# One chain of norms for eight row blocks, begun inside the attention, with new places for some roundings and subtractions, on one Trainium2 core

## The chip, the core and the metric

The kernel runs on one core of a Trainium2 chip. The core has a matrix engine (PE, with a separate row PEld for its weight loads), VectorE (DVE), ScalarE (ACT), GpSimd (POOL) and SyncE (SP), whose queue issues the DMAs. Each engine works through its own list of instructions in order; semaphores make one wait for another. The metric is the device time of one execution in microseconds (us), as the median of several runs. All detailed times come from one execution that the hardware profiler recorded.

## What is computed

One decoder layer on x of 1024 rows by 1024 columns in float32. The change lies where the first half of the layer (mixers and output projection) passes into the second (norm and MLP):

```python
    merged = jax.nn.sigmoid(gate_a) * o_gdn + jax.nn.sigmoid(gate_b) * o_att
    x = x + merged @ w_out

    h2 = rms_norm(x, norm_mlp_g)
    x = x + jnp.square(jax.nn.relu(h2 @ w_mlp_up)) @ w_mlp_down
    return x

def rms_norm(x, g):
    xf = x.astype(jnp.float32)
    y = xf * lax.rsqrt(jnp.mean(xf * xf, axis=-1, keepdims=True) + EPS)
    return (y * g.astype(jnp.float32)).astype(x.dtype)
```

`o_gdn` comes from a gated delta rule and `o_att` from an attention in which each query keeps 256 selected keys; `w_mlp_up` is 1024 by 4096. The gain g of the norm is multiplied into the up weights, so the kernel only scales each row by its root.

## The kernel before

**Row blocks.** The 1024 rows are eight blocks of 128. The attention goes through them in the order 0, 7, 1, 6, 2, 3, 5, 4, each in two groups of four heads (`g` = 0, 1): scores `s` on PE, a softmax on VectorE (`mx`, `nm`, `pr`) and ScalarE (`pr`), transposes `pt` of the probabilities on PE, their rounding into a high part `ph` (ScalarE) and a low part `pl` (VectorE), and the product `o` with the values. The output projection follows each block (PE, name `dd`). `residual` adds it into the block's row buffer, writes the rows to HBM by a DMA on SP's queue (`XD`, 512 KB; the last stage reads them back) and sums the squares on ScalarE.

**Names of buffers.** The row buffers are called `w` with a number: blocks 0, 1, 2, 3 are `w_11064`, `w_11166`, `w_11267`, `w_11327`; blocks 5, 6, 7 are `w_11364`, `w_11207`, `w_11119`; block 4, the last, is `w_11402`. `ident` is the identity for transposes; `pt` and `s` are two rings of two PSUM banks each; `m` are slots of merged activations and weights; `hh` and `ha` are high parts, `hl` and `la` low parts of a rounded operand.

**Norm.** `roots` turns the sum of squares into a reciprocal root with 11 VectorE instructions of one to three elements per partition (`nms`, `nr`, `n2t`): the mean, a first guess and three Newton steps. `norm2` does it for blocks 0, 1, 2 and then for 3, scales each block in place once its XD write is through (the first 512 columns on VectorE, the others on ScalarE), and turns the first half of the rows by eight groups of four transposes, which `norm_out` rounds (`ha`, `la`). `early` does the same for blocks 6, 7 and for 5, and forms on VectorE what a product scheme with seven instead of eight products needs of the second half of the rows (t1 to t4, sums and differences of halves, in place). `early_columns` transposes the columns of blocks 5, 6, 7 for two of these sets, in groups of three, which `early_rounded` rounds with 384 elements. `norm2b` treats block 4: its roots, its parts of t1, t2, t3, and in one go t4 of all four blocks.

**What sets the order.** The program is a set of generators with a priority each (a low number goes first). The planner `Weave` keeps a clock for every engine, adds an assumed cost for each instruction, and steps the best generator whose conditions are met. `yield "V"` means: wait until VectorE is free; `yield ("xd", tb)`: until the planned arrival of that write. The order so planned is fixed for each engine. The first lines of a generator's stretch up to the next `yield` are planned together, and a step's end (`wv.t`) is that of the latest of its instructions. Nearly all instructions are issued by one helper, L2203, so the trace shows one line for all of them, and names have to serve in place of lines. After the last selection of keys the planner also counts the port that VectorE and GpSimd share (`wv.shared`).

Of the kernel before, what the change touches and what calls it, by code (L numbers as in the profile page):

```python
# [14 lines left out]
AF = mybir.ActivationFunctionType  # L15
OP = mybir.AluOpType
# [9 lines left out]
HALF = 512  # L26
# [24 lines left out]
def body(tc, a, out, dbg=None):  # L51
    nc = tc.nc
    ctx = ExitStack()
    V, A, G, PE, SY = nc.vector, nc.scalar, nc.gpsimd, nc.tensor, nc.sync
# [43 lines left out]
    wv = Weave(tc)  # L98
# [3 lines left out]
    def rsq_w(pl, dst, src, n, tag, apart=True):  # L102
        t = pl.tile([P, max(n, 4)], F32, name=tag + "t")[:, :n]
        V_.tensor_scalar(dst.bitcast(I32), src.bitcast(I32), -0.5, float(0x5F3759DF), op0=OP.mult, op1=OP.add)
        for _ in range(3):
            if apart:
                yield
            V_.scalar_tensor_tensor(t, dst, -0.5, src, op0=OP.mult, op1=OP.mult)
            if apart:
                yield  # L110
            V_.tensor_tensor(t, t, dst, op=OP.mult)
            if apart:
                yield
            V_.scalar_tensor_tensor(dst, t, 1.5, dst, op0=OP.add, op1=OP.mult)
# [80 lines left out]
    def after(key):  # L195
        wv.add(0, later(wv.busy["SY"] + SY_LATENCY, key))
# [1216 lines left out]
    def residual(qb, pw):  # L1413
        yield ("x", qb)
        yield 0.2
        for c in range(2):
            cs = slice(c * HALF, (c + 1) * HALF)
            V_.tensor_tensor(x1[qb][:, cs], x1[qb][:, cs], pw[c], op=OP.add)
        yield
        wv.done("x1", qb)  # L1420
        SY_.dma_start(XD[qb * P:(qb + 1) * P, :], x1[qb])
        after(("xd", qb))
        junk = tp.tile([P, D], BF16, name="th", bufs=2)
        A_.activation(junk, x1[qb], AF.Square, accum_out=nss[:, qb:qb + 1])
        yield
        wv.done("ss", qb)
# [9 lines left out]
        yield  # L1436
        wv.done("h2k", half, k)

    def roots(tbs):
        for tb in tbs:  # L1440
            yield ("ss", tb)
        bs = slice(min(tbs), max(tbs) + 1)
        V_.tensor_scalar(nms[:, bs], nss[:, bs], 1.0 / D, EPS, op0=OP.mult, op1=OP.add)
        yield from rsq_w(cst, nr[:, bs], nms[:, bs], len(tbs), "n2", apart=False)
        yield


    def norm2():
        tbs = [qb for qb, g in ATT if g and qb // 4 == first]
        for now in (tbs[:3], tbs[3:]):  # L1450
            yield from roots(now)
            for tb in now:
                yield ("xd", tb)
                for c, eng in enumerate("VA"):
                    yc = x1[tb][:, c * HALF:(c + 1) * HALF]
                    yield eng
                    if c:
                        A_.activation(yc, yc, AF.Copy, scale=nr[:, tb:tb + 1])
                    else:
                        V_.tensor_scalar(yc, yc, nr[:, tb:tb + 1], None, op0=OP.mult)  # L1460
        yield
        for c in range(2):
            ys = [x1[first * 4 + i][:, c * HALF:(c + 1) * HALF] for i in range(4)]
            for k in range(4 * c, 4 * c + 4):
                ring = (ss, ptr)[k % 2]
                yield ring.ready
                ps, slot_ = ring.get()
                for i in range(4):
                    PE_.transpose(ps[:, i * P:(i + 1) * P], ys[i][:, (k % 4) * P:(k % 4 + 1) * P], ident)
                wv.add(1, norm_out(first, k, ps, ring, slot_))  # L1470
            yield
            wv.done("turned", c)
# [5 lines left out]
    y22, comb, pairs = {}, {}, {}  # L1478
    places = {0: 0, 2: 2, 3: 4, 1: 6}

    def early(tbs):
        yield from roots(tbs)
        for tb in tbs:
            i, r = tb % 4, nr[:, tb:tb + 1]
            b11, b12 = part(first, 0)[i], part(1 - first, 0)[i]
            y22[i] = part(1 - first, 1)[i]
            yield ("xd", tb)
            yield "A"
            A_.activation(y22[i], y22[i], AF.Copy, scale=r)
            yield  # L1490
            yield ("turned", 0)
            yield "V"
            V_.scalar_tensor_tensor(b11, b12, r, b11, op0=OP.mult, op1=OP.subtract)
            yield "V"
            V_.scalar_tensor_tensor(b12, b12, r, y22[i], op0=OP.mult, op1=OP.subtract)
            yield
            wv.done("combined", i)

    def early_columns():
        js = [tb % 4 for tb in EARLIER]  # L1500
        for j in js:
            yield ("combined", j)
        yield ("wo", NA - 2)
        for m in (0, 2):
            if m:
                yield
                for j in js:
                    yield "V"
                    V_.tensor_tensor(y22[j], y22[j], part(first, 0)[j], op=OP.subtract)
                yield  # L1510
            for k in range(4):
                if k % 2 == 0:
                    pairs[m, k // 2] = [hpair(f"{n}{places[m] + k // 2}") for n in ("hh", "hl")]
                    for i in range(2):
                        comb[m, k + i] = [t[:, i] for t in pairs[m, k // 2]]
                ring = (ss, ptr)[k % 2]
                yield ring.ready
                ps, slot_ = ring.get()
                for j in js:
                    PE_.transpose(ps[:, j * P:(j + 1) * P], y22[j][:, k * P:(k + 1) * P], ident)  # L1520
                wv.add(2, early_rounded(m, k, ps, ring, slot_))
        yield
        wv.done("early")

    def early_rounded(m, k, ps, ring, slot_):
        cs = slice(min(EARLIER) % 4 * P, (max(EARLIER) % 4 + 1) * P)
# [25 lines left out]
    vl[1] = pA.tile([P, NB, P], F32R, name="vl1")  # L1552
    wv.add(1, vprep(1))
    wv.add(4, score())
    wv.add(0, loadm())
    wv.add(0, loadx())
    wv.add(1, wout_weights())
# [12 lines left out]

    wv.run(until=("pv", NA - 2))
    wv.add(8, norm2())
    for tbs in (EARLIER[1:], EARLIER[:1]):
        wv.add(2, early(tbs))
    wv.add(2, early_columns())


# [99 lines left out]
    def norm2b():  # L1677
        tb = ATT[-1][0]
        i, r = tb % 4, nr[:, tb:tb + 1]
        yield from roots([tb])  # L1680

        y = hpair("hh6", F32)[:, 0]
        t1, t4, t3, t2 = part(first, 0), part(first, 1), part(1 - first, 0), part(1 - first, 1)
        V_.tensor_scalar(y, t2[i], r, None, op0=OP.mult)
        yield
        yield ("early",)
        wv.add(0, last_columns(0, i, y))
        V_.scalar_tensor_tensor(t1[i], t3[i], r, t1[i], op0=OP.mult, op1=OP.subtract)
        yield ("T", 0, 3)
        V_.tensor_tensor(t2[i], y, t1[i], op=OP.subtract)  # L1690
        yield
        wv.add(0, last_columns(2, i, t2[i]))
        V_.scalar_tensor_tensor(t3[i], t3[i], r, y, op0=OP.mult, op1=OP.subtract)
        yield ("T", 2, 3)
        wv.add(1, columns(3, t3))
        yield "V"
        for j in range(4):
            V_.tensor_tensor(t4[j], t4[j], t2[j], op=OP.subtract)
        yield ("col", 3)
        wv.add(1, columns(1, t1))  # L1700
        yield ("col", 1)
        wv.add(1, columns(4, t4))

    def last_columns(m, i, row):
# [480 lines left out]
class _Ordered:  # L2185
# [12 lines left out]
    def __getattr__(self, op):  # L2198
        f = getattr(self.eng, op)
        name, wv = self.name, self.wv  # L2200

        def call(*args, **kw):
            ins = f(*args, **kw)  # L2203
            o = args[0] if args else kw["out"]
            n = 1
            for d in o.shape[1:]:
                n *= d
            if name == "PE":
                fast = op == "matmul" and args[1].dtype == F32R
                if op == "matmul" and not fast and "tile_position" not in kw:  # L2210
                    return wv.issue(name, ins, (n * 1.67 + 5) / 1e3, 0.25)
                if op == "matmul" and "tile_position" in kw:
                    return wv.issue(name, ins, 0.03, 0.25)
                return wv.issue(name, ins, (n * (0.417 if fast else 0.835) + (13.4 if wv.shared else 2.5)) / 1e3, 0.25)
            if name == "SY":
                return wv.issue(name, ins, max(0.5, n * o.shape[0] / 9e4), SY_LATENCY)
            if name == "A":
                return wv.issue(name, ins, 0.13 + n / 1200 + (0.1 if "accum_out" in kw else 0), 0.15)
            if name == "V":
                return wv.issue(name, ins, 0.07 + n / 960, 0.12, self.port(op, args, kw))  # L2220
            if op == "tensor_tensor":
                return wv.issue(name, ins, 0.33 + n / 476, 0.2, True)
            return wv.issue(name, ins, 0.15 + n / 1000, 0.2)
        return call
# [49 lines left out]
```

## Time and profile before

| | |
|---|---|
| median of 3 runs | 1806.71 us (1806.06 to 1808.27) |
| profiled execution | 1806.61 us, its span 1804.9 us |
| mean granted clock of PE | 0.998 of full |
| PE busy | 1783.6 us (99%) |
| VectorE busy | 1287.2 us (71%) |
| ScalarE busy | 1022.8 us (57%) |
| GpSimd busy | 533.3 us (30%) |
| chain that ended last, by engine | PE 93%, DVE 4%, ACT 1%, issue 1%, POOL 1% |

The span is the time from the first to the last recorded instruction; 1.7 us of the execution lie around it. The chain is followed back from the last instruction: at each step to the work that released it. PE is busy nearly throughout, so a gain must either take work off PE or fill the few holes in its list; the holes are found by listing the stretches in which it is idle, with the engine that ended each. Times in the rows below count from the span's start.

### The profile page before, as it was taken

How to read it: one execution, taken by the hardware profiler on the slowest of the kernel's cores; microseconds unless marked ns; L12 is line 12 of the kernel's file. 1: busy time of each engine (PE TensorE's matmuls, PEld its weight loads, DVE VectorE, ACT ScalarE, POOL GpSimd, SP SyncE). 2: the span in 40 equal slices, each digit the busy share in tenths (PEclk: the TensorE clock that was granted, in tenths of full speed). 3: DMA queues.
4: the chain of work that ended last, by engine and by line, in shares of the span. 5: the costliest groups of instructions: out<-in, count | busy, mean ns of one | idle time of the engine just before them, and what ended most of it. 6: DMA issues, size and time to landing. Idle time of an engine off the chain costs nothing.

```text
span 1804.9 us, 28444 instructions
## 1 busy us (share of the span) xinstructions
PE 1783.6 (99%) x10252; PEld 1517.6 (84%) x10252; DVE 1287.2 (71%) x2746; ACT 1022.8 (57%) x2186; POOL 533.3 (30%) x738
## 2 busy tenths in 40 slices
PE   9999999999999999999999999989999999999999
PEld 8999998888888888888888888768888888888887
DVE  5556768867877788875368677776766668969673
ACT  6566656656676554553457666666766664333331
POOL 0003530743362415753014121222323222222230
PEclk9999999999999999999999999999999999999999
DMA  5111242232222222232355221315445459473241
GB/s 165 50 47 47 71 129 65 50 97 77 66 64 71 53 65 69 75 86 75 95 186 183 76 90 53 114 38 184 167 152 170 135 185 363 133 250 122 100 136 52
DMA packets 192193, 198.80 MB, mean 110 GB/s; under 512 B 36738, under 2 KB 140467, under 8 KB 192051
## 3 DMA queue, kind: packets, MB, share of 16 engines
q1 hardware_dynamic: 192050, 196.97, 34.7%
q8 instruction: 81, 1.33, 0.3%
q14 instruction: 62, 0.50, 0.1%
HBM read 141.20 MB, written 55.74 MB: 109 GB/s over the span
## 4 chain that ended last, share of the span: by engine, by line
PE 93%; DVE 4%; ACT 1%; issue 1%; POOL 1%; DMA 0%; SPq 0%; ACTq 0%; POOLq 0%; DVEq 0%
PE dd L2203 55%; PE o L2203 15%; PE s L2203 7%; PE pt L2203 6%; PE tt L2203 3%; PE cc L2203 2%; PE sq L2203 2%; PE oo L2203 1%; PE jj L2203 1%; DVE w L2203 1%; DVE hl L2203 1%; DVE m L2203 0%; PE tp L2203 0%; DVE n2t L2203 0%; DMA pj<-in_x_dram 0%
## 5 line engine op out<-in xcount | busy, mean ns | idle before, releaser
L2203 PE MATMUL dd<-hh,w 128*128 128x512 f32 x1568 | 517.4, 401 | 0.0
L2203 PEld LDWEIGHTS dd<-hh,w 128*128 128x128 f32 x1568 | 289.0, 189 | 51.4
L2203 PE MATMUL dd<-hl,w 128*128 128x512 f32 x784 | 316.2, 403 | 0.9 <-DVE hl L2203 0.9
L2203 ACT ACTIVATE m<-m 128x512 f32<-128x512 f32 (+1 forms) x240 | 139.9, 625 | 79.3 <-PE dd L2203 34.3
L2203 PE MATMUL dd<-w,hh 128*128 128x256 f32 x960 | 179.4, 284 | 0.4 <-DVE w L2203 0.4
L2203 PE MATMUL dd<-hh,m 128*128 128x512 f32 x520 | 173.5, 398 | 0.7 <-DVE w L2203 0.5
L2203 DVE TENSOR_TENSOR m<-m,m 128x512 fp32r<-128x512 f32 (+2 forms) x184 | 143.3, 804 | 38.7 <-ACT m L2203 33.3
L2203 PEld LDWEIGHTS dd<-hl,w 128*128 128x128 f32 x784 | 147.8, 189 | 26.4 <-DVE hl L2203 1.4
L2203 PEld LDWEIGHTS dd<-w,hh 128*128 128x128 f32 x960 | 151.5, 191 | 1.5 <-DVE w L2203 0.6
L2203 PE MATMUL dd<-w,hl 128*128 128x256 f32 x480 | 136.2, 284 | 0.0
L2203 POOL TENSOR_TENSOR sx<-sx,stmp 128x60 f32<-128x60 f32 (+24 forms) x248 | 119.7, 483 | 19.4
L2203 PEld LDWEIGHTS dd<-hh,m 128*128 128x128 f32 x520 | 97.6, 190 | 20.4 <-DVE w L2203 2.0
L2203 POOL TENSOR_TENSOR stmp<-sx,um 128x60 f32<-128x60 f32 (+24 forms) x186 | 83.4, 448 | 89.5 <-DMA um<-ZA 61.8
L2203 POOL TENSOR_TENSOR m<-m,m 128x512 f32<-128x512 f32 x48 | 69.0, 1445 | 120.6 <-DVE m L2203 63.3
L2203 PE MATMUL dd<-hl,m 128*128 128x512 f32 x260 | 103.2, 397 | 0.9 <-POOL hl L2203 0.9
L2203 DVE TENSOR_SCALAR_CACHE_REDUCE tkeq<-sc,cand 128x384 f16<-128x384 f32 (+3 forms) x128 | 103.3, 807 | 1.0
L2203 ACT ACTIVATE hh<-m 128x1024 fp32r<-128x1024 f32 x44 | 45.1, 1056 | 90.0 <-PE s L2203 42.0
L2203 ACT ACTIVATE ha<-m 128x1024 fp32r<-128x1024 f32 x44 | 45.3, 1056 | 86.0 <-PE o L2203 34.9
L2203 PEld LDWEIGHTS dd<-w,hl 128*128 128x128 f32 x480 | 91.8, 191 | 0.6
L2203 DVE TENSOR_TENSOR w<-w,w 128x1024 fp32r<-128x1024 f32 (+1 forms) x63 | 71.0, 1130 | 22.5 <-ACT w L2203 21.7
L2203 ACT ACTIVATE tkcm<-sc,cand 128x896 f16<-128x896 f32 x64 | 70.0, 1094 | 28.3 <-DVE cand L2203 25.2
L2203 ACT ACTIVATE w<-w 128x1024 fp32r<-128x1024 f32 x48 | 50.8, 1058 | 53.9 <-PE dd L2203 53.7
(413 smaller groups left out, 4412.2 us busy)
## 6 DMA issues: line engine op xcount, KB each, us to landing
HD<-m SPq DMA_DIRECT2D x112, 256.0 KB, 2.3
m<-HD SPq DMA_DIRECT2D x56, 512.0 KB, 3.9
w<-in_w_in_dram SPq DMA_DIRECT2D x48, 512.0 KB, 4.0
m<-in_w_mlp_up_dram SPq DMA_DIRECT2D x33, 512.0 KB, 4.8
wraw<-in_w_in_dram SPq DMA_DIRECT2D x8, 1024.0 KB, 5.3
m<-in_w_mlp_down_dram SPq DMA_DIRECT2D x16, 512.0 KB, 7.4
w<-in_x_dram SPq DMA_DIRECT2D x10, 512.0 KB, 5.5
es<-GC SPq DMA_DIRECT2D x8, 512.0 KB, 4.9
```

What stands on the lines that cost most here:

```text
L2203: ins = f(*args, **kw)
```

## The change

- A new generator `norms` makes the roots of all blocks in one chain, in the order of the attention: (0, 7), (1, 6), (2, 3), (5). It is added with the attention itself, with priority 2. For the first two groups (`apart`) each of the small instructions is planned by itself, so that others can stand between them; `norm2b` still makes block 4's.
- A new generator `scaled` for each block scales both halves in place (the first 512 columns only for blocks 0 to 3) as soon as its roots are there and its XD write has arrived.
- `norm2` and `early` no longer make roots or scale; they wait for `("scaled", tb)`. `early` is now one generator per block, in the order 7, 6, 5.
- `early_rounded` has priority 0 in place of 2.
- t4 of blocks 5, 6, 7 is formed at the end of `early_columns`; `norm2b` forms block 4's alone, and later, behind set 1's transposes.
- In `residual` the planned end of a step no longer includes the issue of the XD write.
- In the planner, a VectorE instruction of under 16 elements per partition is put at 0.17 us plus its elements, not 0.07, while the port is shared.

The number of instructions is the same on every engine.

```diff
+        t = wv.t
         SY_.dma_start(XD[qb * P:(qb + 1) * P, :], x1[qb])
         after(("xd", qb))
+        wv.t = t
...
-    def roots(tbs):
+    def roots(tbs, apart=False):
...
-        bs = slice(min(tbs), max(tbs) + 1)
+        bs = slice(tbs[0], tbs[-1] + 1, max(1, tbs[-1] - tbs[0]))
...
+    def norms():
+        qbs = [qb for qb, g in ATT if g]
+        for n, grp in enumerate((qbs[0:2], qbs[2:4], qbs[4:6], qbs[6:7])):
+            yield from roots(sorted(grp), apart=n < 2)
+            for tb in grp:
+                wv.add(2, scaled(tb))
+
+    def scaled(tb):
+        yield ("xd", tb)
+        r = nr[:, tb:tb + 1]
+        for c, eng in enumerate("VA"):
+            yc = x1[tb][:, c * HALF:(c + 1) * HALF]
+            if eng == "A":
+                yield eng
+                A_.activation(yc, yc, AF.Copy, scale=r)
+            elif tb // 4 == first:
+                yield eng
+                V_.tensor_scalar(yc, yc, r, None, op0=OP.mult)
+        yield
+        wv.done("scaled", tb)
...
-                wv.add(2, early_rounded(m, k, ps, ring, slot_))
+                wv.add(0, early_rounded(m, k, ps, ring, slot_))
...
+        for j in js:
+            yield ("turned", 1)
+            yield "V"
+            t4 = part(first, 1)[j]
+            V_.tensor_tensor(t4, t4, y22[j], op=OP.subtract)
+        yield
+        wv.done("early", 4)
...
+    wv.add(2, norms())
...
-        yield "V"
-        for j in range(4):
-            V_.tensor_tensor(t4[j], t4[j], t2[j], op=OP.subtract)
         yield ("col", 3)
         wv.add(1, columns(1, t1))
         yield ("col", 1)
+        yield ("early", 4)
+        yield "V"
+        V_.tensor_tensor(t4[i], t4[i], t2[i], op=OP.subtract)
+        yield
         wv.add(1, columns(4, t4))
...
-                return wv.issue(name, ins, 0.07 + n / 960, 0.12, self.port(op, args, kw))
+                return wv.issue(name, ins, (0.17 if n < 16 and wv.shared else 0.07) + n / 960, 0.12, self.port(op, args, kw))
```

On VectorE, where the last block's softmax meets the first norms, the order before has both Newton chains ahead of the softmax's `mx` (these are their last rows):

```order
L2203 TENSOR_TENSOR n2t<-n2t,nr 128x3
L2203 SCALAR_TENSOR_TENSOR nr<-n2t,nr 128x3
L2203 RECIPROCAL mx<-nm 128x1
L2203 TENSOR_SCALAR w_11064<-w_11064,nr 128x512
L2203 TENSOR_SCALAR w_11166<-w_11166,nr 128x512
L2203 TENSOR_TENSOR pl<-pt,ph 128x512 x2
```

The same place in the changed kernel:

```order
L2219 SCALAR_TENSOR_TENSOR nr<-n2t,nr 128x2
L2219 RECIPROCAL mx<-nm 128x1
L2219 TENSOR_SCALAR nm<-mx 128x1
L2219 TENSOR_TENSOR pl<-pt,ph 128x512
L2219 ISA pr,mx<-s,mk 128x512
L2219 ISA mx 128x1
L2219 ISA pr,mx<-s,mk 128x128
L2219 ISA mx 128x1
L2219 TENSOR_TENSOR pl<-pt,ph 128x512
L2219 TENSOR_SCALAR w_11267<-w_11267,nr 128x512
L2219 TENSOR_SCALAR nm<-mx 128x1
```

One chain of 11 instructions (blocks 2 and 3) stands here now in place of two, and the scalings of blocks 0 and 1 have gone earlier.

On PE at the same place, before: the transposes of the last block's probabilities between products of the output projection.

```order
L2203 MATMUL dd<-hl_11114,m_12977 128x512
L2203 MATMUL dd<-hh_11113,m_12977 128x512 x2
L2203 MATMUL pt<-ident,pr 128x128 x8
L2203 MATMUL dd<-hl_11114,m_12977 128x512
L2203 MATMUL dd<-hh_11113,m_12977 128x512
```

And now (the last of seven such groups of four ahead of `pt<-ident,pr`):

```order
L2219 MATMUL dd<-hl_11114,m_12910 128x512
L2219 MATMUL s<-ident,w_11064 128x128
L2219 MATMUL s<-ident,w_11166 128x128
L2219 MATMUL s<-ident,w_11267 128x128
L2219 MATMUL s<-ident,w_11327 128x128
L2219 MATMUL pt<-ident,pr 128x128 x4
L2219 MATMUL dd<-hh_11113,m_12910 128x512
```

Seven of the eight groups of transposes of blocks 0 to 3 have moved ahead of these transposes of probabilities.

On VectorE behind block 4's Newton chain, before: the scaling of block 4 first, four other instructions on slots `m`, a combination, and then the first low part of blocks 5 to 7.

```order
L2203 SCALAR_TENSOR_TENSOR nr<-n2t,nr 128x1
L2203 TENSOR_SCALAR hh_13674<-w_11402,nr 128x512
L2203 TENSOR_TENSOR m_13595<-m_13472,m_13595 128x512
L2203 TENSOR_TENSOR m_13615<-m_13615,dd 128x512
L2203 SCALAR_TENSOR_TENSOR w_11064<-w_11402,nr,w_11064 128x512
L2203 TENSOR_TENSOR m_13663<-m_13473,m_13663 128x512
L2203 TENSOR_TENSOR m_13679<-m_13476,m_13679 128x512
L2203 TENSOR_TENSOR hl_13640<-s,hh_13639 128x384
```

And now:

```order
L2219 SCALAR_TENSOR_TENSOR nr<-n2t,nr 128x1
L2219 TENSOR_TENSOR hl_13591<-s,hh_13590 128x384
L2219 TENSOR_TENSOR hl_13591<-pt,hh_13590 128x384
L2219 TENSOR_TENSOR hl_13601<-s,hh_13600 128x384
L2219 TENSOR_TENSOR hl_13601<-pt,hh_13600 128x384
L2219 TENSOR_TENSOR m_13616<-m_13505,m_13616 128x512
L2219 TENSOR_TENSOR w_11267<-w_11267,w_11207 128x512
L2219 TENSOR_SCALAR hh_13673<-w_11402,nr 128x512
L2219 TENSOR_TENSOR m_13656<-m_13656,dd 128x512
L2219 SCALAR_TENSOR_TENSOR w_11064<-w_11402,nr,w_11064 128x512
```

The four low parts (the second half's first sets) stand ahead of block 4's scaling; `w_11267<-w_11267,w_11207` is one of the t4 subtractions, which before stood together, four in a row, further down.

## Rows read from the trace of the kernel before

**Rows 1.** Busy time of each engine by stretch; PEclk is PE's granted clock.
```profile
core 0: us, PE busy (x) PEld busy (x) DVE busy (x) ACT busy (x) POOL busy (x), PEclk, DMA share, GB/s
980.00:1130.00 150.00, 149.91 (x817) 127.22 (x816) 106.72 (x317) 93.76 (x187) 27.33 (x21) 1.00 0.22 70
1140.00:1150.00 10.00, 6.89 (x31) 5.49 (x29) 5.33 (x20) 6.90 (x14) 1.29 (x1) 0.83 0.21 73
1180.00:1190.00 10.00, 6.76 (x36) 5.59 (x35) 7.98 (x20) 7.68 (x22) 4.15 (x3) 0.92 0.00 1
1220.00:1600.00 380.00, 379.99 (x1677) 314.43 (x1676) 279.41 (x352) 223.69 (x393) 104.79 (x63) 1.00 0.54 184
...
1200.00:1220.00 20.00, 17.43 (x99) 13.94 (x98) 15.15 (x22) 12.09 (x23) 2.23 (x2) 1.00 0.14 51
1130.00:1220.00 90.00, 80.37 (x403) 65.19 (x402) 69.62 (x154) 59.34 (x122) 23.38 (x17) 0.96 0.25 82
1174.00:1186.00 12.00, 11.19 (x54) 8.72 (x53) 11.34 (x24) 11.97 (x32) 6.62 (x5) 1.00 0.12 47
```

**Rows 2.** Timeline of PE, 1132 to 1219: start, us, instruction, [idle before it, what ended it].
```profile
1143.54 0.84 PE L2203 MATMUL pt<-ident,pr 128*128 128x128 f32 x5 [3.11 <-ACT pr L2203]
1162.39 0.50 PE L2203 MATMUL dd<-hh,m 128*128 128x512 f32 x1 [0.53 <-DVE w L2203]
1188.51 1.09 PE L2203 MATMUL s<-ident,hh 128*128 128x128 f32 x4 [3.24 <-DVE hl L2203]
1206.47 0.66 PE L2203 MATMUL s<-ident,w 128*128 128x128 f32 x4 [1.23 <-DVE hl L2203]
```

**Rows 3.** Chain of waits, 1124 to 1220: start, us, engine and output.
```profile
1124.44 0.87 PE pt L2203 x8
...
1144.38 4.72 PE dd L2203 x14
...
1189.60 3.41 PE o L2203 x10
1193.01 4.55 PE dd L2203 x20
...
1201.75 3.46 DVE w L2203 x4
```

**Rows 4.** Timeline of VectorE, ScalarE and GpSimd at the first hole.
```profile
1137.52 1.22 DVE L2203 TENSOR_SCALAR nr<-nms 128x2 int32<-128x2 int32 x1
1138.77 0.16 DVE L2203 SCALAR_TENSOR_TENSOR n2t<-nr,nms 128x2 f32<-128x2 f32 x1
...
1142.46 0.16 DVE L2203 RECIPROCAL mx<-nm 128x1 f32<-128x1 f32 x1
...
1142.65 0.83 ACT L2203 ACTIVATE pr<-pr,mx 128x640 f32<-128x640 f32 x1 [1.40 <-DVE mx L2203]
...
1137.41 1.29 POOL L2203 TENSOR_TENSOR sg<-sg,m 128x512 f32<-128x512 f32 x1
```

**Rows 5.** Timeline of VectorE ahead of the second hole.
```profile
1181.62 1.20 DVE L2203 TENSOR_TENSOR n2t<-n2t,nr 128x1 f32<-128x1 f32 x1
...
1183.64 0.48 DVE L2203 TENSOR_SCALAR hh<-w,nr 128x512 f32<-128x512 f32 x1
...
1187.82 0.55 DVE L2203 TENSOR_TENSOR hl<-s,hh 128x384 fp32r<-128x384 f32 x1
```

**Rows 6.** VectorE by shape, 1080 to 1220: count, busy us, mean ns, idle before.
```profile
L2203 DVE SCALAR_TENSOR_TENSOR w<-w,nr,w 128x512 f32<-128x512 f32 x4 | 3.7, 919 | 0.0
...
L2203 DVE TENSOR_TENSOR la<-s,ha 128x512 fp32r<-128x512 f32 x4 | 2.7, 682 | 0.3 <-ACT ha L2203 0.3
```

**Rows 7.** SP's queue: waits from 900 to 1230 (total, times, longest), and XD's landing times.
```profile
SPq L2203 <- POOL m L2203: 91.2, 13, 16.3
...
DMA to landing us min/median/max: 3.1/4.3/4.5
```

More of the change, by code (lines that the diff above doesn't have):

```diff
@@ L1437, in norm_out @@
         wv.done("h2k", half, k)
-    def roots(tbs):
+    def roots(tbs, apart=False):
         for tb in tbs:
             yield ("ss", tb)
-        bs = slice(min(tbs), max(tbs) + 1)
+        bs = slice(tbs[0], tbs[-1] + 1, max(1, tbs[-1] - tbs[0]))
         V_.tensor_scalar(nms[:, bs], nss[:, bs], 1.0 / D, EPS, op0=OP.mult, op1=OP.add)
-        yield from rsq_w(cst, nr[:, bs], nms[:, bs], len(tbs), "n2", apart=False)
+        yield from rsq_w(cst, nr[:, bs], nms[:, bs], len(tbs), "n2", apart=apart)
         yield
-    def norm2():
[L1449 to L1461, printed above, removed]
+    def norms():
[17 more added lines that the diff above has]
+        wv.done("scaled", tb)
+    def norm2():
+        for tb in range(first * 4, first * 4 + 4):
+            yield ("scaled", tb)
         for c in range(2):
@@ L1479, in body, with early @@
     places = {0: 0, 2: 2, 3: 4, 1: 6}
[L1481 to L1491, printed above, removed]
-            yield "V"
[L1493 to L1497, printed above, removed]
+    def early(tb):
+        i, r = tb % 4, nr[:, tb:tb + 1]
+        b11, b12 = part(first, 0)[i], part(1 - first, 0)[i]
+        y22[i] = part(1 - first, 1)[i]
+        yield ("scaled", tb)
+        yield ("turned", 0)
+        yield "V"
+        V_.scalar_tensor_tensor(b11, b12, r, b11, op0=OP.mult, op1=OP.subtract)
+        yield "V"
+        V_.scalar_tensor_tensor(b12, b12, r, y22[i], op0=OP.mult, op1=OP.subtract)
+        yield
+        wv.done("combined", i)
     def early_columns():
@@ L1520, in early_columns @@
                     PE_.transpose(ps[:, j * P:(j + 1) * P], y22[j][:, k * P:(k + 1) * P], ident)
-                wv.add(2, early_rounded(m, k, ps, ring, slot_))
+                wv.add(0, early_rounded(m, k, ps, ring, slot_))
         yield
         wv.done("early")
+        for j in js:
+            yield ("turned", 1)
+            yield "V"
+            t4 = part(first, 1)[j]
+            V_.tensor_tensor(t4, t4, y22[j], op=OP.subtract)
+        yield
+        wv.done("early", 4)
     def early_rounded(m, k, ps, ring, slot_):
@@ L1572, in body @@
     wv.add(8, norm2())
-    for tbs in (EARLIER[1:], EARLIER[:1]):
-        wv.add(2, early(tbs))
+    for tb in EARLIER[::-1]:
+        wv.add(2, early(tb))
     wv.add(2, early_columns())
@@ L1695, in norm2b @@
         wv.add(1, columns(3, t3))
-        yield "V"
-        for j in range(4):
-            V_.tensor_tensor(t4[j], t4[j], t2[j], op=OP.subtract)
         yield ("col", 3)
@@ L1701, in norm2b @@
         yield ("col", 1)
+        yield ("early", 4)
+        yield "V"
+        V_.tensor_tensor(t4[i], t4[i], t2[i], op=OP.subtract)
+        yield
         wv.add(1, columns(4, t4))
```

## The prediction, made before the changed kernel had run

> **What bounds the kernel now.** I read the busy times by stretch first [rows 1]. PE works 149.91 of the 150 us from 980 to 1130 and 379.99 of the 380 from 1220 to 1600; only from 1130 to 1220 does it stand idle, 90 - 80.37 = 9.6 us. That is the passage from the attention to the MLP, where the change lies. The timeline of PE [rows 2] says where: at A (1143.54) 3.11 us for the last block's softmax, at B (1162.39) 0.53 for the residual of the next block, at C (1188.51) 3.24 for a low part `hl`, and in D, from 1200 to 1220, 20 - 17.43 = 2.57, of which the one of 1.23 is listed. Together 9.45 of the 9.6.
>
> The two long holes cost more than their length, because PE runs slower afterwards: the granted clock is 0.83 in the stretch of A and 0.92 in that of C, but 1.00 after D's 1.23 us [rows 1, 2]. A share between the two levels, 1.2 and 2.4 GHz, means that part of the stretch ran at the lower. In the chain [rows 3] 14 `dd` after A take 4.72 us (337 ns each), 20 at full clock 4.55 (227.5 each): 14 x 0.11 = 1.5 us lost. Ten `o` after C take 3.41: 3.41 - 10 x 0.2275 = 1.1. The transposes that end the holes are slow too: eight at full clock take 0.87 (0.109 each), five at A 0.84 (0.3 lost), four at C 1.09 (0.65 lost).
>
> So the holes' cost is A 3.11 + 1.5 + 0.3 = 4.9, B 0.5, C 3.24 + 1.1 + 0.65 = 5.0, D 2.6: **13.0 us**. A second way confirms the size: between 1124.3 and 1218.6 I counted 267 matmuls of 512 columns, 9 of 256 and 152 transposes in the trace, 60.7 + 1.0 + 16.6 = 78.3 us of work at full clock in 94.3 us, so 16.0 lost; 3 us lie in gaps too short for the list.
>
> **Why they are there.** At A [rows 4] VectorE makes two Newton chains, 22 small instructions, from 1137.3 to 1142.46, ahead of the softmax's reciprocal `mx`; ScalarE's `pr` then starts at 1142.65 and PE at 1143.54. The small instructions take 0.16 us each and follow each other at (1142.46 - 1138.77) / 20 = 0.185. The first guess took 1.22, beside a GpSimd instruction of 1.29 that began just before. At C [rows 5] block 4's chain ends at 1183.6, and then come its scaling, four instructions on `m` and a combination before the `hl` at 1187.82 that PE needs. VectorE and ScalarE are nearly full there: 11.34 and 11.97 of the 12 us from 1174 [rows 1]. In D the four t4 subtractions take 3.46 us in one go [rows 3], just ahead of the wait of 1.23.
>
> **The change part by part.**
>
> Place A. Of 22 small instructions ahead of `mx` 11 go; 11 x 0.185 = 2.0 us of VectorE, and with the 1.0 us that the blocked first guess cost, 3 of the 5 us are open to saving. The order also puts seven groups of four transposes (7 x 4 x 0.109 = 3.05 us of PE work) ahead of the last block's `pt<-ident,pr`, so PE has work while VectorE makes the remaining chain (11 x 0.185 = 2.0). The hole for the softmax should go. Late next is the seventh group: each ring has two banks, and this group needs the bank that the second low part of its ring frees. Ahead of that VectorE has two low parts of 0.682, two combinations of 0.919 and the low part itself [rows 6], 3.9 us, while PE has five groups and three products, 5 x 0.436 + 3 x 0.2275 = 2.9. That leaves a wait of about 1.0; with two or three shorter ones for the residual and the probabilities, 0.8, I keep 1.8. The bounds are 0 (VectorE a little early) and the old 4.9. No hole is as long as 3 us, so the slow clock goes too; D's 1.23 at clock 1.00 is the nearest row. A regains 4.9 - 1.8 = 3.1.
>
> Place B. The residual still waits for the product and PE for the residual: 0.5 stays.
>
> Place C. The low parts of 384 elements (0.55 each) stand directly behind the chain now. By before's clock the first ends at 1183.64 + 0.55 = 1184.2 instead of 1188.4, 4.2 us earlier; the hole is 3.24. Late next is block 4's scaling `hh`, now behind four low parts and two instructions of about 0.9, 4 x 0.55 + 1.8 = 4.0 later than before, with PE's products of the MLP as cover. The bounds are 0 and 3.24; the margin of the first wait is only 4.2 - 3.24 = 1, so I take 0.9, nearer to zero. ScalarE must make the high parts first; the new priority puts them ahead there as well. Regained 5.0 - 0.9 = 4.1.
>
> Place D. Three of the four t4 subtractions leave it (3.46 x 3 / 4 = 2.6 us of VectorE) and the fourth moves behind set 1. VectorE was busy 15.15 of the 20 us and ScalarE 12.09 [rows 1], so without the three there is room. The subtractions go to places ahead of and in C, where they are part of the 0.9. I keep 0.4; bounds 0 and 2.6. Regained 2.2.
>
> Moved into the attention: two chains of 11 (22 x 0.185 = 4.1 us of VectorE, and about 1 us more for each instruction that meets GpSimd) and the scalings of four blocks. I cost them at nothing on PE: VectorE is busy 106.7 of 150 us there, ScalarE 93.8, GpSimd 27.3 [rows 1], and for the first two groups the instructions are spread singly. Without that cover it would be 4.1 plus up to 2.
>
> The other edits have no price of their own: the planner's cost of small instructions only moves the order, and keeping the XD issue out of a step's end lets the square be planned sooner.
>
> A rule of the Trainium skill speaks against this cover. The rows first: the first guess beside GpSimd took 1.22 us and a product of two small operands 1.20, the other small ones 0.16 [rows 4, 5]. "SBUF — State Buffer", section "Who interferes with whom", says that VectorE and GpSimd share a pair of ports as an exclusive lock, and that a VectorE instruction with two inputs in SBUF contends with a GpSimd instruction that reads. By that rule every chain that meets GpSimd pays about 1 us, wherever it stands; the chain still ahead of `mx` would pay it at A and the sum would be 8.4 instead of 9.4. The rows agree with the rule in two of three chains looked at, and I keep 9.4, as that microsecond lies under the seven groups.
>
> Sum: 3.1 + 0 + 4.1 + 2.2 = 9.4 us, all after 1130. Against the profiled execution (1806.6, its span 1804.9 and 1.7 around it) that is **1797.2 us**. The median of the runs, 1806.7, differs from it by 0.1, so the number stands for the median too.
>
> **The rivals.**
>
> *Only A is regained.* At C and D VectorE and ScalarE are the bound, not their order: 11.34 and 11.97 of 12 us busy. The change removes no instruction, and the t4 subtractions of two blocks go into this very stretch. Then C keeps its hole and its slow clock, D goes half: 3.1 + 1.3 = 4.4, **1802.2 us**. For it: the fill. Against it: ScalarE's list there holds work for the MLP's products that PE doesn't wait for, and C's wait is for one early `hl` behind instructions that nobody waits for.
>
> *The holes move and are not filled.* The seven groups of transposes wait for their banks one by one, because the low parts stand behind softmax instructions; PE then stands 3 us at A as before and the clock falls again, and D alone gains, with 1 us of C: 3.2, **1803.4 us**. For it: PE's transposes (0.436 a group) are quicker than a low part (0.682). Against it: four groups need no bank back.
>
> *Slower: the scaling in place waits for the XD write.* It may only overwrite a block when the write has read it. SP issues XD in order, behind loads into slots that GpSimd frees, and its waits for GpSimd reach 16.3 us; a write lands 4.3 us after its issue [rows 7]. The scaling stands in VectorE's and ScalarE's lists ahead of softmax steps and holds them up. Followed through the new order, block 3's write lands some 2 us before its scaling comes up; it stands behind the last block's two loads. If SP were late by the longest wait, the stop would be 16.3 - 2 = 14.3, and with the slow clock after it (1.5) the time 1797.2 + 15.8 = **1813 us**. It becomes slower than before by 0.2% from a delay of 2 + 13.0 - 1.5 = 13.5 us. Against it: the same two loads were issued before XD in the old order as well, and with no such wait there.
>
> *More than forecast.* All 13.0 go and a third of the short gaps (1.0): **1792.6 us**.
>
> **How the numbers follow.** Chances: forecast (with its own bounds, 1793.5 to 1801) 0.60; only A 0.17; moved 0.11; slower 0.05; more 0.07. A measurement of this kernel can tell about 0.2%, 3.6 us, from no change: faster means below 1803.1, slower above 1810.3. The forecast, "more", nearly all of "only A" and a third of "moved" are faster: 0.60 + 0.07 + 0.13 + 0.03 = 0.83. The rest of these two is the same, 0.12, and the last rival is slower, 0.05. The range for 8 in 10 leaves out the slower case, two thirds of "moved" and half of "more": 1792.5 to 1803.
>
> **What would show it.** In the changed kernel's trace: no hole above 1.5 us between 1130 and 1220, the granted clock 1.00 in all its stretches, PE idle there some 3 to 4 us instead of 9.6, and the end of this passage about 9 us earlier with 1220 to 1600 unchanged in length. A hole that ends in `hl` with a clock below 1.00 near 1180 would show "only A"; one before `s<-ident,w` that ends in `la` shows "moved"; one that ends in a VectorE scaling, with SP waiting for GpSimd, the slower case. PE idle between 880 and 1130 would show that the attention didn't cover the chains. Wrong altogether would be a gain with the holes still there.

## The result: 0.9936 of the time before

The changed kernel takes 1796.01 us (median of 5 runs, 1794.89 to 1796.54) against 1807.31 (5 runs, 1806.06 to 1808.27): a ratio of 0.9936 with a 95% interval of 0.9924 to 0.9947. The profiled span went from 1804.9 to 1793.8 us, by 11.1. The forecast was 1797.2, 9.4 us less than before; the total came out 1.2 us lower and inside the range (before's median is 0.6 us higher beside this run, so the gain is 11.3 by medians). For part of it the reasons were wrong, as the experiments show.

The busy times by stretch of the changed kernel, as in [rows 1] (PE, PEld, DVE, ACT, POOL, then PE's clock, the DMAs' share and GB/s):

```profile
980.00:1130.00 150.00, 149.91 (x812) 126.55 (x811) 107.41 (x332) 95.45 (x188) 27.41 (x21) 1.00 0.23 71
...
1140.00:1150.00 10.00, 8.87 (x59) 7.28 (x58) 7.71 (x14) 7.67 (x17) 1.51 (x1) 1.00 0.16 53
...
1180.00:1190.00 10.00, 10.00 (x47) 8.09 (x46) 10.00 (x14) 8.33 (x20) 6.45 (x5) 1.00 0.07 27
...
1220.00:1600.00 380.00, 379.40 (x1675) 313.87 (x1674) 276.88 (x350) 224.91 (x391) 107.25 (x64) 1.00 0.55 187
...
1130.00:1220.00 90.00, 88.77 (x463) 73.48 (x462) 75.25 (x148) 61.30 (x128) 24.61 (x17) 1.00 0.32 106
1174.00:1186.00 12.00, 12.00 (x56) 9.71 (x55) 11.65 (x26) 12.00 (x31) 6.28 (x4) 1.00 0.10 37
```

PE now stands idle 90 - 88.77 = 1.2 us in the passage, not 9.6, and the clock is 1.00 throughout. With the slow instructions that [rows 3] showed (3.55 us in all) that is 8.4 + 3.55 = 11.95. The MLP gives 0.6 back: 379.40 busy of 380 against 379.99. That leaves 11.35, against 11.1 in the span.

The timeline of PE has two holes above 0.5 us from 1130 to 1600 (start, us, instruction, [idle before, what ended it]):

```profile
1145.10 0.63 PE L2219 MATMUL s<-ident,w 128*128 128x128 f32 x4 [1.13 <-DVE la L2219]
...
1501.68 0.50 PE L2219 MATMUL pt<-hl,hh 128*128 128x512 f32 x1 [0.60 <-DVE hl L2219]
```

The first is the one that the prediction left at A, at the instruction and behind the low part that it named: the seventh group, for which it worked out 1.0 us. VectorE shows the two combinations ahead of that low part, and its own wait for a high part ahead of the first low part:

```profile
1141.74 0.69 DVE L2219 TENSOR_TENSOR la<-s,ha 128x512 fp32r<-128x512 f32 x1 [0.92 <-ACT ha L2219]
1142.35 0.68 DVE L2219 TENSOR_TENSOR la<-pt,ha 128x512 fp32r<-128x512 f32 x1
1142.94 1.40 DVE L2219 SCALAR_TENSOR_TENSOR w<-w,nr,w 128x512 f32<-128x512 f32 x2
1144.27 0.68 DVE L2219 TENSOR_TENSOR la<-s,ha 128x512 fp32r<-128x512 f32 x1
```

The second is new, in the MLP: the chain of waits leads from it through a load of down weights of 7.5 us back to a write of 5.5.

```profile
1486.20 5.48 DMA HD<-m
...
1491.75 7.53 DMA m<-in_w_mlp_down_dram
...
1500.39 1.24 DVE hl L2219
```

The transposes of the first half of the rows, and those of blocks 5 to 7, begin earlier; before (PE):

```profile
1157.39 0.60 PE L2203 MATMUL s<-ident,w 128*128 128x128 f32 x4
...
1171.37 0.49 PE L2203 MATMUL s<-ident,w 128*128 128x128 f32 x3
```

and in the changed kernel:

```profile
1140.47 0.60 PE L2219 MATMUL s<-ident,w 128*128 128x128 f32 x4
...
1165.96 0.49 PE L2219 MATMUL s<-ident,w 128*128 128x128 f32 x3
```

At C and in D no wait is left, although ScalarE fills 12.00 and VectorE 11.65 of the 12 us from 1174, more than before. But the transposes of block 4 start just where their input ends (VectorE, then PE):

```profile
1180.18 1.52 DVE L2219 TENSOR_SCALAR hh<-w,nr 128x512 f32<-128x512 f32 x1
...
1181.85 0.63 PE L2219 MATMUL s<-ident,hh 128*128 128x128 f32 x4
...
1190.08 1.78 DVE L2219 TENSOR_TENSOR w<-hh,w 128x512 f32<-128x512 f32 x1
...
1191.96 0.63 PE L2219 MATMUL s<-ident,w 128*128 128x128 f32 x4
```

The scaling ends at 1181.70 and PE takes it at 1181.85; the difference of two halves ends at 1191.86 and PE takes it at 1191.96. That nothing waits there isn't a sign of slack (d_chain measures it).

### The profile page after: what moved, and what is told of

It is laid out like the page before. It is cut to its first block, busy times and chain, and to the rows that moved or that the text cites. A ratio compares the mean times of both kernels' runs of the same rounds, so it can differ in the third digit from the quotient of the medians.

```text
span 1793.8 us, 28449 instructions
## 1 busy us (share of the span) xinstructions
PE 1780.3 (99%) x10252; PEld 1515.6 (84%) x10252; DVE 1284.5 (72%) x2746; ACT 1022.6 (57%) x2186; POOL 536.1 (30%) x738
## 5 line engine op out<-in xcount | busy, mean ns | idle before, releaser
L2219 ACT ACTIVATE m<-m 128x512 fp32r<-128x512 f32 (+1 forms) x240 | 139.9, 625 | 78.8 <-PE o L2219 29.7
```

## The experiments

All kernels compute the whole layer; they move instructions, or do a few of them twice. Each was timed beside the kernel before on the same chip. The chips' times of before are 1807.3, 1807.25, 1808.0 and 1807.15, so the table compares by the ratio to before, and gives the us below before. An interval reaches some 2.2 us to either side, so two rows less than about 3 us apart are not told apart by their times alone; for those the holes in the traces are the evidence.

| kernel | what differs | median us | ratio (95%) | us below before |
|---|---|---|---|---|
| changed | | 1796.01 | 0.9936 (0.9924 to 0.9947) | 11.3 |
| u_prio | old priority of early_rounded | 1796.76 | 0.9942 (0.9929 to 0.9956) | 10.5 |
| u_t4 | four t4 subtractions together | 1796.62 | 0.9941 (0.9928 to 0.9953) | 10.6 |
| u_cost | old cost in the planner | 1795.63 | 0.9935 (0.9922 to 0.9947) | 11.6 |
| u_late | chain of norms at its old place | 1806.03 | 0.9993 (0.9984 to 1.0002) | 1.2 |
| a_norms | the early chain alone, on the kernel before | 1798.48 | 0.9945 (0.9932 to 0.9957) | 9.5 |
| s_hold | chains early, scalings at their old place | 1801.82 | 0.9965 (0.9952 to 0.9977) | 6.1 |
| d_chain | ten more small instructions for block 4 | 1798.56 | 0.9950 (0.9937 to 0.9964) | 9.4 |
| b_stt | combinations behind all transposes | 1799.07 | 0.9949 (0.9937 to 0.9962) | 8.9 |
| u_keep | XD issue counted in residual's step | 1801.29 | 0.9970 (0.9960 to 0.9981) | 5.9 |
| u_apart | first two chains planned in one piece | 1808.03 | 1.0003 (0.9994 to 1.0012) | -0.9 |
| d_cover | two chains in the attention done thrice | 1801.21 | 0.9964 (0.9952 to 0.9977) | 5.9 |
| d_xd | block 3's XD written twice | 1796.51 | 0.9942 (0.9929 to 0.9956) | 10.6 |

### Which part did it: undo one at a time

**u_prio**

```diff
-                wv.add(0, early_rounded(m, k, ps, ring, slot_))
+                wv.add(2, early_rounded(m, k, ps, ring, slot_))
```

> The changed kernel with early_rounded back at priority 2; all else as changed. Theory 'each part fills its own hole': the new priority filled C, so the hole of about 3 us before s<-ident,hh that ends in DVE hl comes back with its slow clock, 5.0 us in all: about 1801 us against 1796. Rival 'the early start did it all': the roots, scalings and transposes that come earlier leave VectorE room at C whatever the priority, so the time stays within 1 us of 1796 and PE has no hole above 1 us there.

0.8 us came back, within the intervals, and no hole at C: C is clear without the priority. The low parts do not even stand behind block 4's chain here; the last of the four (VectorE) is just ahead of the chain's first instruction:

```profile
1178.60 0.54 DVE L2219 TENSOR_TENSOR hl<-pt,hh 128x384 fp32r<-128x384 f32 x1
1179.07 0.14 DVE L2219 TENSOR_SCALAR nms<-nss 128x1 f32<-128x1 f32 x1
```

What is new is a hole of 1.09 at 1253.92, in the MLP.

**u_t4**

```diff
-        yield ("early", 4)
-        yield "V"
-        V_.tensor_tensor(t4[i], t4[i], t2[i], op=OP.subtract)
+        for j in range(4):
+            V_.tensor_tensor(t4[j], t4[j], t2[j], op=OP.subtract)
```

(with the loop at the end of early_columns taken out, and the four subtractions ahead of set 3's transposes as before)

> The changed kernel with the four t4 subtractions together in norm2b again; all else as changed. Theory 'each part': D's holes come back, 2.6 us, the largest of them (1.2 us) right behind the four subtractions of 3.5 us: about 1798.6 us. Rival 'the early start': by then nothing waits on VectorE for long, under 0.7 us comes back: 1796 to 1796.7.

0.7 us came back, within the intervals, and one hole of 0.81 in D in place of 2.57: standing together, the t4 subtractions account for about a third of D's holes.

**u_cost**

```diff
-(0.17 if n < 16 and wv.shared else 0.07) + n / 960
+0.07 + n / 960
```

> The changed kernel with the planner's old cost of small VectorE instructions (0.07 us plus elements); the work is the same, only the order moves. Theory 'each part': the cost has no place of its own, 1796 plus or minus 1. Rival 'zero margin': in the changed trace the transposes of block 4 (1181.85) start 0.1 us after the scaling that they wait for ends, because the planner now knows how long the 11 small instructions take; at the old cost it thinks them 11 x 0.1 = 1.1 us shorter and sets these transposes too early, so holes of about 1 us come back at two or three places: 1798 to 1799 us.

No difference; one new hole of 0.53. My second theory was wrong here: with the old cost the order differs and so do its tight places.

**u_late**

```diff
-    wv.add(2, norms())
...
+    wv.add(2, norms())
     wv.add(8, norm2())
```

> The changed kernel with the chain of norms added only where norm2 and early are added (behind the last but one row block), all else as changed. Theory 'each part': A comes back, 3.11 us and its slow clock, while C and D stay filled: 1800 to 1801 us. Rival 'the early start did it all': A, C and D all come back, 9 us or more: 1805 us or more.

The gain is gone but for 1.2 us (the interval includes none), although priority, t4, planner's cost and the rest are as changed. The holes are not at their old places (timeline of PE):

```profile
1168.98 0.66 PE L2219 MATMUL s<-ident,w 128*128 128x128 f32 x4 [1.59 <-DVE la L2219]
1173.65 0.97 PE L2219 MATMUL pt<-ident,w 128*128 128x128 f32 x4 [3.32 <-DVE la L2219]
...
1202.03 0.63 PE L2219 MATMUL s<-ident,hh 128*128 128x128 f32 x4 [1.41 <-DVE hl L2219]
```

The softmax no longer makes one, as the order puts it ahead; the roundings of the transposes do, with four chains of norms among them. At `s<-ident,hh`, which is C, 1.41 is back. This isn't the order before with the other edits added, though: one chain makes the blocks in turn, block 3 third (at 1157.43, before at 1152.79), and the first transposes begin at 1165.48, 8.1 us later than before.

### The early start: alone, and split

**a_norms** (the kernel before with `norms`, `scaled`, the new `roots` and `early` by blocks, without the other edits; the piece of the diff that makes the difference)

```diff
     wv.add(4, score())
+    wv.add(2, norms())
```

> The early start alone: the kernel before with the chain of norms begun in the attention, the scalings behind it and early by blocks; the old priority of early_rounded, the t4 subtractions together, the old planner's cost and the old end of residual's step. Theory 'the early start did it all': nearly the whole gain, 1796 to 1797.5 us. Rival 'it needs one of the others': of the three small edits taken singly each cost under 1 us, but together they could be worth the 5 us of C: 1800 us or more, with a hole of about 3 us near 1180.

9.5 of the 11.3 us. Between the two theories, nearer to the first: the largest hole is 1.64 at 1150.63, none at C, and 1.05 in D. The four low parts end here at 1179.34, ahead of block 4's chain (1179.55), as in u_prio.

**s_hold**

```diff
     def scaled(tb):
+        yield ("pv", NA - 2)
         yield ("xd", tb)
```

> The changed kernel with the chains early as they are, but every scaling (and with it the transposes, combinations and roundings) held until the last but one row block is done, where norm2 and early were added before. Theory 'the small instructions': what filled the holes is that 33 Newton instructions, 33 x 0.19 = 6 us of VectorE, left the crowded stretch: 1796 to 1797.5 us. Rival 'the scalings': what counts is that the row blocks are ready, so that transposes and their roundings start earlier: at least half of the gain goes, 1801 us or more, with holes that end in DVE la or hl.

6.1 us below before. Between u_late (1.2) and the changed kernel (11.3) this splits the way: 4.9 us go with the chains of small instructions that are done by then, 5.2 with the scalings and what follows them. Both theories hold one half; it is a split of the way from u_late, whose order is worse than before's.

Where the 5.2 are lost matters. The largest holes end in a low part of the probabilities and in residuals, not in `la` or `hl` as the rival said (2.21 and 2.26; then 1.23 behind a residual, and 0.94 and 0.35 in D):

```profile
1148.35 0.94 PE L2220 MATMUL pt<-ident,w 128*128 128x128 f32 x4 [2.21 <-DVE pl L2220]
...
1163.29 0.50 PE L2220 MATMUL dd<-hh,m 128*128 128x512 f32 x1 [2.26 <-DVE w L2220]
...
1171.40 0.49 PE L2220 MATMUL s<-ident,w 128*128 128x128 f32 x3
...
1185.62 0.60 PE L2220 MATMUL s<-ident,hh 128*128 128x128 f32 x4
```

C (the last line) has no wait, although the transposes of blocks 5 to 7 begin at 1171.40, no earlier than before. VectorE has the low parts directly behind block 4's scaling:

```profile
1181.63 0.48 DVE L2220 TENSOR_SCALAR hh<-w,nr 128x512 f32<-128x512 f32 x1
1182.03 0.55 DVE L2220 TENSOR_TENSOR hl<-s,hh 128x384 fp32r<-128x384 f32 x1
```

**u_keep**

```diff
-        t = wv.t
         SY_.dma_start(XD[qb * P:(qb + 1) * P, :], x1[qb])
         after(("xd", qb))
-        wv.t = t
```

> The changed kernel with residual's planned step ending again only with the issue of the XD write; the work is the same, only the order moves. Theory 'a small edit': like the other three, under 1 us: 1796 to 1797. Rival 'it starts the chain': with it the square of a block is planned 1.5 us sooner, and so all roots, scalings and transposes; without it part of the early start goes, and with it up to half of what holding the scalings cost, 2 us or more: 1798 or more.

5.4 us came back. SP's timeline shows block 5's XD write and what is ahead of it, first here and then in the changed kernel:

```profile
1137.12 25.65 SPq L2217 DMA_DIRECT2D m<-in_w_mlp_up_dram  x7
1162.86 0.53 SPq L2217 DMA_DIRECT2D XD<-w  x1
```

```profile
1136.86 0.92 SPq L2219 DMA_DIRECT2D m<-in_w_mlp_up_dram  x2
1159.39 0.34 SPq L2219 DMA_DIRECT2D XD<-w  x1
1159.82 5.17 SPq L2219 DMA_DIRECT2D m<-in_w_mlp_up_dram  x5
```

Seven loads instead of two stand ahead of it. Block 5's square ran at 1159.37, but its chain of norms comes only at 1170.49, behind the next block's residual (1169.20), against 1160.58 in the changed kernel. The transposes of blocks 5 to 7 follow at 1185.50 (there 1165.96), and PE waits 1.88, 0.47 and 1.30 us between 1194 and 1200 for high and low parts. So the price isn't that of an instruction: the edit changes only what the plan takes for the end of a step, here the issue of a write behind seven loads. (The planner's own times are not in the traces; that they moved the chain is read from the code and the order.)

**u_apart**

```diff
-            yield from roots(sorted(grp), apart=n < 2)
+            yield from roots(sorted(grp), apart=False)
```

> The changed kernel with the small instructions of the first two chains planned in one piece instead of one by one. Theory 'cover': a piece of 11 x 0.19 = 2.1 us of VectorE fits into the attention, where PE has no hole, so 1796 plus or minus 0.7 and no hole before 1130. Rival 'spread needed': the piece holds up a softmax and PE waits up to 2 us twice: 1798 to 1800.

The whole gain is gone, more than either theory said. What the piece itself costs is one hole in the attention, behind the 11 small instructions of the first chain (PE):

```profile
1011.19 0.50 PE L2219 MATMUL s<-kTh,qh 128*128 128x512 f32 x1 [1.10 <-DVE mx L2219]
```

That is the rival's mechanism, at one place of two. The other holes, 9.2 us in all from 1130 to 1220, are in the passage again (three of six; another, 1.68 at 1185.10, is C):

```profile
1160.76 0.50 PE L2219 MATMUL dd<-hh,m 128*128 128x512 f32 x1 [2.00 <-DVE w L2219]
1174.50 0.50 PE L2219 MATMUL dd<-ha,m 128*128 128x512 f32 x1 [1.20 <-DVE w L2219]
...
1191.70 0.73 PE L2219 MATMUL dd<-ha,m 128*128 128x512 f32 x2 [1.86 <-DVE m L2219]
```

Between the two the order of the attention has drifted apart: the residual of block 2 comes at 1104.82, in the changed kernel at 1094.72, that of block 3 at 1137.60 against 1131.04, and the transposes of blocks 0 to 3 begin at 1151.83 against 1140.47. Why planning 22 small instructions in two pieces shifts the projections by 7 to 10 us stays open; no run separates it.

### Costs by themselves

**d_chain**

```diff
+        if again:
+            wv.blind = True
+            yield from rsq_w(cst, nr[:, bs], nms[:, bs], len(tbs), "n2", apart=apart)
+            wv.blind = False
```

(in `roots`, with `again` set for block 4 alone; `wv.blind`: the planner counts these instructions at nothing, so the order of all others stays)

> The changed kernel with ten small instructions of block 4's chain done a second time (the same values again), without the planner knowing, so the order of all else stays. Theory 'zero margin': the transposes s<-ident,hh of block 4 start 0.1 us after their scaling, so 10 x 0.195 = 1.95 us more of VectorE show on PE nearly whole, as one hole of 1.8 to 2 us that ends in DVE hh: 1797.8 to 1798 us. Rival 'cover' (the prediction's view, a margin of about 1 us at C): about 1 us, 1797.

```profile
1184.74 0.63 PE L2223 MATMUL s<-ident,hh 128*128 128x128 f32 x4 [1.85 <-DVE hh L2223]
```

1.95 us more on VectorE make 1.85 on PE, and the time is 1.9 us further from the changed kernel's (9.4 below before against 11.3). The margin at C is 0.1 us, as good as none.

**b_stt**

```diff
         yield ("scaled", tb)
-        yield ("turned", 0)
+        yield ("turned", 1)
```

> The changed kernel with the combinations of early waiting for all eight groups of transposes (turned, 1) and not for the first four. Theory 'the two combinations make A's last hole': the low part that the seventh group waits for no longer stands behind 1.4 us of combinations, so the hole of 1.13 goes: 1794.9 us. Rival 'moved again': the combinations, 1.4 us of VectorE, then stand nearer to C, where VectorE is full and the margin is zero, and the hole comes back there: 1796 us or more.

A's hole shrinks to 0.21 as the first theory says, and the rival is right about the time, 2.4 us less gain, but not about the place: C stays clear. The holes are now 0.76 and 0.31 behind residuals (B had been closed), 0.24, and 1.0 in D, 2.5 us with A's against 1.1; the rest of the 2.4 lies within the intervals:

```profile
1144.60 0.66 PE L2219 MATMUL s<-ident,w 128*128 128x128 f32 x4 [0.21 <-DVE la L2219]
...
1159.51 0.50 PE L2219 MATMUL dd<-hh,m 128*128 128x512 f32 x1 [0.76 <-DVE w L2219]
...
1202.57 0.63 PE L2219 MATMUL pt<-ident,w 128*128 128x128 f32 x4 [0.80 <-DVE hl L2219]
```

**d_cover**

```diff
-            yield from roots(sorted(grp), apart=n < 2)
+            yield from roots(sorted(grp), apart=n < 2, again=n < 2)
```

(`again`: the chain done twice more at its end, with `wv.blind`)

> The changed kernel with the chains of (0, 7) and (1, 6) done twice more (the same values), 20 small instructions or 3.8 us of VectorE in one piece at two places of the attention, without the planner knowing, so that the order of all else stays. Theory 'cover' (the prediction's term of nothing): hidden, at most 0.7 us: 1796 to 1797. Rival 'no cover': PE waits for the softmax behind them, up to 3.8 us at each place and the slow clock after it, 1798 to 1805.

```profile
1020.94 0.50 PE L2224 MATMUL o<-pl,vh 128*128 128x512 f32 x1 [1.68 <-DVE pl L2224]
...
1083.57 0.50 PE L2224 MATMUL s<-kTh,qh 128*128 128x512 f32 x1 [1.83 <-DVE mx L2224]
```

Of 3.8 us at each place about 2 are hidden and 1.7 to 1.8 show. The rest of the 5.4 is slow clock behind the second hole: the eight transposes at 1084.37 take 1.76 us against 0.87 in [rows 3], and the granted clock from 1080 to 1090 is 0.83. The attention's cover is some 2 us at a place, not without bound.

**d_xd**

```diff
         SY_.dma_start(XD[qb * P:(qb + 1) * P, :], x1[qb])
+        if qb == 3:
+            wv.blind = True
+            SY_.dma_start(XD[qb * P:(qb + 1) * P, :], x1[qb])
+            wv.blind = False
```

> The changed kernel with block 3's XD write issued a second time (the same rows), behind the first one's end, without the planner knowing. It measures the slower rival: its write is issued at 1133.7 and takes 4.4 us, the scaling comes up at about 1139. With the second write the end moves by 4.4 us to some 1142.5. Theory 'the scaling waits, and all behind it': a hole of 2.5 to 3.5 us before the first s<-ident,w, behind a VectorE or ScalarE scaling, with a slow clock after it: 1799 to 1801. Rival 'covered': VectorE and ScalarE have little behind the scaling that PE needs at once, and A's last hole of 1.13 takes part of it up: under 1 us, 1796 to 1797.

The waits are where the slower rival put them, on ScalarE and VectorE:

```profile
1140.57 0.72 ACT L2223 ACTIVATE w<-w,nr 128x512 f32<-128x512 f32 x1 [2.07 <-DMA XD<-w]
```

```profile
1140.59 0.49 DVE L2223 TENSOR_SCALAR w<-w,nr 128x512 f32<-128x512 f32 x1 [1.66 <-DMA XD<-w]
```

The second write ended about 3 us after the first, sooner than I had put it, and PE lost 0.44 of the 1.7 to 2.1 (1141.13). In the changed kernel itself no scaling waits for XD.

## Why the prediction was right, and where not

**What bounds the kernel, and the clock's part: right.** The gain is the holes plus the slow instructions behind them, 11.95 us by the same count, and the attention's and nearly all of the MLP's stretches have not changed. The second count was misread: it left 3 us "in gaps too short for the list", but [rows 1] has 9.6 us of idle time and 9.45 of it is in the holes named. The 3 us are not gaps but busy time that the count at full clock doesn't hold; the rival "more" took a third of them for a gain.

**A: right in mechanism and size.** 1.8 us were to stay, 1.0 of them for the seventh group; 1.13 stayed there, and 0.15 for its slower first group (0.59 us from its start to the next group's, against 0.44). The shorter waits (0.8) did not come. That 1.13 is so near to 1.0 is partly luck: from the first low part on VectorE took 3.2 us, not 3.9 (the two combinations 1.40 together, not 1.84), and PE had 2.2 us of work left, not 2.9, since VectorE had first waited 0.92 for ScalarE's high part, which the sum left out.

**B: mis-sized, a little.** 0.5 was kept; the hole is gone, since the order puts other products there.

**C and D: the total nearly right, the causes in part wrong.** I kept 0.9 and 0.4 and nothing stayed; these terms, with B's, are why the forecast was 1.8 us of gain too low. The step that failed is the one that tied each hole to one edit: C to the priority that puts the low parts directly behind block 4's chain, D to the t4 subtractions that leave. With either edit undone, C and D stay filled to within 0.8 us; a_norms has neither and no hole at C; and with both there and the chain at its old place (u_late), 10 of the 11.3 us are gone and C waits 1.41. So the early start is enough for C without the priority: the low parts then stand even ahead of block 4's chain.

Which part of the early start does it is only partly shown. It isn't simply that the transposes come sooner: s_hold holds the scalings back, its transposes of blocks 5 to 7 begin at 1171.40 (before 1171.37), and C is empty all the same, with the low parts where the prediction wanted them, behind block 4's scaling. s_hold keeps the new priority, so no run has the chains early, the scalings late and the old priority, and what fills C there is not separated. D is less sensitive than C but not indifferent to t4: 0.81 is back in u_t4, 1.05 in a_norms, 1.3 in s_hold. That the total of C and D came out near the forecast owes something to luck, since the edits to which it was put down could go singly at 0.7 to 0.8 us each.

**"Moved into the attention, at nothing": right for this kernel, for a narrower reason.** 149.91 of 150 us of PE as before. But d_cover finds cover for 2 us at a place and u_apart a hole of 1.10 behind one of its two pieces of 11. The attention's share of idle VectorE time, from which I argued, doesn't say what fits at one place; spread one by one the chains fitted everywhere.

**"The other edits have no price of their own": wrong.** For the planner's cost it held (0.3 us the other way, within the intervals). Leaving the XD issue out of a step's end is worth 5.4 us in this kernel, and planning in single instructions 12.2, of which only the hole of 1.10 is explained. They aren't terms that can be summed, though: a_norms lacks the first and still gains 9.5.

**The port rule.** The prediction weighed "SBUF — State Buffer", section "Who interferes with whom", of the Trainium skill: about 1 us for a chain that meets GpSimd. In the changed kernel the chain of blocks 2 and 3 met none and ran at 0.16 to 0.17 an instruction; block 5's met two (0.52 at 1160.96 and 1.22 at 1162.29) and block 4's one. The trace agrees with the rule in these: the VectorE instruction has two inputs and ends with the GpSimd instruction beside it, within 0.03 us.

```profile
1174.77 0.88 DVE L2219 SCALAR_TENSOR_TENSOR n2t<-nr,nms 128x1 f32<-128x1 f32 x1
```

```profile
1174.02 1.61 POOL L2219 TENSOR_TENSOR m<-m 128x512 f32<-128x512 f32 x1 [0.69 <-DVE m L2219]
```

Two rows are no clear case of it as the prediction put it, for two inputs. The first guess of 1.22 in [rows 4] reads one tensor, so one of the prediction's three chains agrees plainly, not two. Block 4's scaling reads one tensor and one value for each row; it took 1.52 us against 0.48 in [rows 5], beside two GpSimd instructions from 1179.80 to 1182.85. There the scaling stood on the zero margin and cost PE nothing only because the order had placed the transposes behind it.

**The rivals.** "Only A" rested on VectorE and ScalarE being full at C; they are fuller now (11.65 and 12.00 of 12 us) and PE doesn't wait. "The holes move": false for the change itself, but true for b_stt, u_late and u_keep. The slower one: its wait exists, and d_xd shows a delay of 2 us costing 0.44.

## What to carry to other kernels

When the order of all engines is planned ahead, a hole on the engine that bounds need not belong to the instruction that ended it: price a reordering by when its inputs are ready in the whole passage, and undo each edit singly before giving it a share. A place without a wait is not a place with slack; compare the end of the input with the start of its user. Small instructions can hide in a busy engine's stretch when they are spread one by one; here 11 in one piece showed at one of two places (1.10 us), 20 in one piece at both (1.68 and 1.83).

## What the runs showed that I had not expected

- Short holes can slow PE as a long one does. In u_keep 1.88, 0.47 and 1.30 us fall between 1194 and 1200, and the next stretch runs at a granted clock of 0.83, that is at 1.2 in place of 2.4 GHz for part of the time. Whether the three together did it or the longest alone is not separated:

```profile
1190.00:1200.00 10.00, 6.35 (x34) 4.90 (x33) 8.61 (x17) 5.60 (x12) 0.91 (x1) 1.00 0.14 53
1200.00:1210.00 10.00, 10.00 (x49) 8.35 (x48) 4.99 (x10) 4.67 (x10) 0.00 (x0) 0.83 0.00 0
```

- Holes of the same length do not cost the same: 1.85 us in d_chain left the clock at 1.00 in its own stretch and the next, 1.83 in d_cover brought it to 0.83, while 1.68 at d_cover's other place left it at 1.00. No run shows what makes the difference.
- An edit of two lines in what the planner takes for a step's end (u_keep) moved the time as much as half of the whole change.
